# Score bursts of two head pairs, an earlier Exp table load, one maximum per head and another list order in a two-layer encoder kernel

## Chip, cores and metric

The kernel runs on one core of a Trainium2 chip. The metric is the device time of one execution in microseconds (us); lower is better.

## What is computed

Two layers, each a mixer and a channel part, on x of 256 tokens by 1024 features, in float32. The mixer has 16 heads of width 64 in three kinds: four neighbourhood heads ("a", with a relative position bias), six dilated window heads ("d") and six heads ("c") that share two key and value heads.

```python
def mixer_sublayer(x, n1, w_in_l, qg, kg, rpb_l, og, w_out_l, tables):
    h = rms_norm(x, n1)
    proj = h @ w_in_l                         # 1024 x 2560
    qa, ka, va, qd, kd, vd, qc, kc, vc = jnp.split(proj, cuts, axis=-1)
    # q and k: rms_norm per head, rotary positions for d and c
    out_a = neighbourhood_attention(...)
    out_d = dilated_window_attention(...)
    out_c = gqa_block_attention(...)
    mix = concatenate([rms_norm(out_a), rms_norm(out_d), rms_norm(out_c)])
    return x + mix @ w_out_l                  # 1024 x 1024

def channel_sublayer(x, n2, w_gu, cw, cb, w_dn):
    h = rms_norm(x, n2)
    g, u = jnp.split(h @ w_gu, 2, axis=-1)    # 1024 x 5632
    g = depthwise_conv_centred(g, cw, cb)     # width 3 along the tokens
    return x + (jax.nn.gelu(g) * u) @ w_dn    # 2816 x 1024

for l in range(2):
    x = mixer_sublayer(...)
    x = channel_sublayer(...)
```

## The kernel before

Tokens lie on the 128 partitions in two tiles (t = 0, 1); their transposes, features on partitions, are what TensorE multiplies. Every float32 product is three matmuls (`mm3`): each operand is split into a high and a low part, and high·high, high·low and low·high are added up in PSUM. So each weight that arrives (`wp_raw`) is cast to its high part by ScalarE (`wp_hi`) and subtracted to its low part by VectorE (`wp_lo`) before TensorE can use it. Weights come in units of up to 2048 columns; four raw buffers and two pairs of parts exist. The first unit u0 of layer 0 comes in four slices w0 to w3 of 128 features each, the second in two halves u1a and u1b of 256 features (together the eight k-steps of the first group of projections), u2 and u3 whole. x comes in five pieces: x(k, n) is the feature blocks k to k+n-1 for all tokens, and x(0,1) and x(1,1) go by ScalarE's queue. Everything else goes by SyncE's (SP's) queue, in the order in which SP issues it.

Stages of a layer: transposes of x into `act_hT` (scaled by the norm's gain, split by ScalarE and VectorE, the form with two operands on VectorE being the low part), the projections in groups (dq, dk, ... into the four PSUM tiles `psa_a`), sums of squares per head (`act_s2k` from `psa_a`, `small_ss`), rotary positions, then the heads. A head's steps are: scores into one PSUM tile "w" of 256 keys for both token tiles (the pool `psw` has four such tiles), a maximum (VectorE), Exp with a row sum (ScalarE), the transposes of p back through `psw`, a split into `act_ch` and `act_cl`, and the weigh step against `const_v`. Scores of two heads are computed in one burst, one head on the lower 64 rows of the array and one on the upper (`scores`, with `nc.together()`: nothing may come between). Projections of later groups are woven in as filler. Then come the three group norms (`act_sqm` is transposed for their sums), the output matrix with `act_mixT_hi` and `act_mixT_lo`, and the addition to `const_x`. The channel part walks through eleven steps of gate (G), up (U) and down; four PSUM tiles `dacc[t][h]` gather the down products for token tile t and column half h, and the last addition writes x out. At the start TensorE multiplies some constants (`const_warm`) while it waits.

No instruction is issued where it is written. `Plan.add` records each operation, and `Plan.order` then sets the order of the whole program by list scheduling: it follows estimated durations (`cost`), estimated DMA times and buffer handovers, and always takes the operation that can start earliest, with ties by rank. The rank is the recorded position, plus shifts of whole sections (`later`), plus an entry of the table `PLACES` for single operations. The first thirteen DMAs, those of the list `START`, have fixed landing times in the table `LANDS`, which are taken by their recorded position:

```python
o.rank = i + self.shift + PLACES.get(i, 0)
...
if i < self.first_loads:
    end = LANDS[sum(p.method == "dma_start" for p in ops[:i])]
```

`not_before(engine)` records that an operation must stand behind the last one recorded so far on that engine. Since all are issued in one helper, every line of the trace is L470; tiles tell the operations apart.

Of the kernel before, what the change touches and what calls it, by code (L numbers as in the profile page):

```python
# [224 lines left out]
def handover(a, b):  # L225
# [1 line left out]


PLACES = {
# [5 lines left out]
}  # L235


class Plan:
    def __init__(self, tc):
        self.tc, self.ops, self.shift, self.burst, self.bursts, self.behind = tc, [], 0, None, {}, None  # L240
# [28 lines left out]
    def add(self, engine, method, args, kw):  # L269
# [49 lines left out]
    def order(self):  # L319
# [79 lines left out]
        while len(done) < len(ops):  # L399
            best = None  # L400
            for e, r in ready.items():
                for i in r:
                    o = ops[i]
                    if e in opened:
                        if o.burst != opened[e]:
                            continue
                        at = at_of(o)
                    elif o.burst is not None:
                        at = at_of_burst(o.burst) if i == self.bursts[o.burst][0] else None
                    else:  # L410
# [25 lines left out]
            if o.method == "dma_start":  # L436

                ring = e if i < self.first_loads else "SP"
                end = max(at + 1360, wires.get(ring, 0.0))
                shared = 0.0  # L440
                if i < self.first_loads:
                    shared = o.size if ring == "ACT" else min(o.size, 120 * max(0.0, wires.get("ACT", 0.0) - end))
                if e == "POOL":
                    end += 1000
                wires[ring] = end + shared / 120 + (o.size - shared) / (280 if i < self.first_loads else 335)
                end = wires[ring] + 1200
                if i < self.first_loads:
                    end = LANDS[sum(p.method == "dma_start" for p in ops[:i])]
            for t in o.tiles:
# [23 lines left out]
def cost(engine, method, args, kw, ins):  # L473

    out = args[0]
    if method == "dma_start":
        w = out if isinstance(out, View) else args[1]
        small = min(out.shape[-1], args[1].shape[-1]) < 128
        spread = isinstance(args[1], bass.AP) and args[1].ap[0][0] == 0
        size = 4 * math.prod(w.shape) * (2 if small else 2 if spread else 1)  # L480
# [34 lines left out]
def encoder_kernel(  # L515
# [72 lines left out]

    minus_half = const.tile([P, 32], F32, tag="mh", name="minus_half")
    nc.gpsimd.memset(minus_half, -0.5)  # L590


    vown, vkv = (
# [281 lines left out]
    for l in range(DEPTH):  # L875
# [181 lines left out]
        class Head:  # L1057
# [4 lines left out]
            def softens(self, sps):  # L1062
# [142 lines left out]
        def na_bias(h):  # L1205

            flat = nabs[l].rearrange("p r c -> p (r c)")
            return [flat[:, (h * RPB_ROWS + 3 - 2 * t) * GRID_W :][:, :S] for t in range(NT)]

        def scores(i):  # L1210

            two = heads[i : i + 2]
            sps = [psw.tile([P, NT, S], F32, tag="w", name=f"s_{z.name}") for z in two]
            g = two[0].group
            with nc.together():
                for t in range(NT):
                    for x, y in ((0, 0), (0, 1), (1, 0)):
                        for z, sp, rows_ in zip(two, sps, (LOW, HIGH)):
                            nc.tensor.matmul(
                                sp[:, t], turned[g + "q"][x][rows_, z.h // 2, t * P : (t + 1) * P],  # L1220
                                turned[g + "k"][y][rows_, z.kv if g == "c" else z.h // 2],
                                start=(x, y) == (0, 0), stop=(x, y) == (1, 0),
                            )
            for z, sp in zip(two, sps):
                z.softens([sp[:, t] for t in range(NT)])

        heads = []
        for h in range(H_DIL):
# [144 lines left out]
        def gate(s):  # L1373
# [28 lines left out]
        def down(steps):  # L1402
            ws = [unit() for _ in steps]
            for h in range(2):
                hs = slice(h * 512, (h + 1) * 512)
                for t in range(NT):
                    c = slice(t * P, (t + 1) * P)
                    for s, (wh, wl) in zip(steps, ws):
                        ch, cl = ready[s]
                        for j in range(2):  # L1410
                            mm3(
                                dacc[t][h], ch[:, j, c], cl[:, j, c], wh[:, j, hs], wl[:, j, hs],
                                s == 0 and j == 0, s == STEPS - 1 and j == 1,
                            )

        last = []
        NA_STEPS = {2: na_load, 3: na_repeat, 4: na_diagonals}
# [19 lines left out]
        for h in range(2):  # L1437
            for t in range(NT):
                hs = slice(h * 512, (h + 1) * 512)
                nc.vector.scalar_tensor_tensor(  # L1440
                    xs[:, t, hs], dacc[t][h], r2[:, t : t + 1], xs[:, t, hs], ALU.mult, ALU.add
                )
                if l == DEPTH - 1:
                    nc.sync.dma_start(ov[:, t, hs], xs[:, t, hs])
    nc.emit()


# [67 lines left out]
```

## Time and profile before

| | before |
|---|---|
| median of 3 runs | 614.73 us (614.57 to 614.73) |
| profiled execution | 614.38 us, span 612.6 us |
| granted TensorE clock, mean | 1.00 |
| layer 0: start, mixer, channel | 0 to 13.9, to 122.3, to 309.7 us |
| layer 1: mixer, channel, tail | to 423.2, to 608.6, to 612.6 us |
| TensorE (PE) busy | 604.5 us |
| VectorE (DVE), ScalarE (ACT) busy | 485.4, 428.5 us |
| GpSimd (POOL) busy | 84.3 us |

The profile is one execution; its span is the time from the first to the last recorded instruction. A row of a timeline gives the start, the duration, the engine, the operation with its output and inputs, shapes, and in brackets the idle time before it with what ended it. A row that stands for several instructions has their count at its end (x8) and the time from the first's start to the last's end. A row of windows gives the window, its length, the busy time of PE, PEld (weight load), DVE, ACT and POOL with counts, the granted clock, the share of DMA time and GB/s. Groups have count, busy us, mean ns and idle us. "SPq" is SyncE's issue of a DMA.

### The profile page before, as it was taken

To read this page: it belongs to the slowest core of one execution; us is meant where nothing else is said; L and a number is where in the kernel's file an instruction comes from. 1 tells how busy PE (TensorE), PEld (TensorE's weight loads), DVE (VectorE), ACT (ScalarE), POOL (GpSimd) and SP (SyncE) were. 2 spreads that over 40 slices of the span, in tenths; PEclk is the share of its full clock that TensorE was granted. 3 is DMA by queue.
4 is the path that set the end of the run, shared out by engine and by line. 5 is a ranking of instruction groups with operands and counts; after the bars stand their busy time and mean duration, and the time that the engine had idled before them with its cause. 6 is when DMAs were issued, how large, how long until landed. Compare 5 with 4: busy or idle time off the path is not lost.

```text
span 612.6 us, 9883 instructions
## 1 busy us (share of the span) xinstructions
PE 604.5 (99%) x3484; PEld 525.2 (86%) x3484; DVE 485.4 (79%) x1000; ACT 428.5 (70%) x1064; POOL 84.3 (14%) x136
## 2 busy tenths in 40 slices
PE   8999999999999999999999999998999999999997
PEld 6998888888888888888899989887888888888885
DVE  4899989797788988887777788767877777777774
ACT  6789999696565766675588889857755656566661
POOL 2732130202400000000032214231000000000000
PEclk9999999999999999999999999999999999999999
DMA  8893403557589799987555626654665555556501
GB/s 272 294 294 141 139 25 105 184 159 242 166 225 326 247 360 326 349 293 251 155 155 182 215 70 240 206 178 129 202 217 179 175 197 201 167 185 205 189 18 68
DMA packets 85073, 121.44 MB, mean 198 GB/s; under 512 B 9864, under 2 KB 69608, under 8 KB 85024
## 3 DMA queue, kind: packets, MB, share of 16 engines
q1 hardware_dynamic: 82752, 112.17, 56.6%
q0 software_dynamic: 1728, 8.39, 4.0%
q8 instruction: 27, 0.44, 0.3%
q10 hardware_dynamic: 544, 0.26, 0.2%
q14 instruction: 22, 0.18, 0.1%
HBM read 110.93 MB, written 9.88 MB: 197 GB/s over the span
## 4 chain that ended last, share of the span: by engine, by line
PE 92%; DVE 2%; ACT 2%; POOL 1%; DMA 1%; issue 1%; SPq 0%; DVEq 0%; POOLq 0%
PE psw_w L470 51%; PE psa_a L470 41%; DMA const_x<-in_x_dram 1%; ACT act_s2k L470 1%; POOL small_rstd L470 1%; DVE const_x L470 1%; DVE wp_lo L470 1%; SPq L470 0%; DVE act_sw L470 0%; DVE act_z L470 0%; ACT wp_hi L470 0%; POOL small_ms L470 0%; ACT L470 0%; ACT act_z L470 0%; ACT act_hT L470 0%
## 5 line engine op out<-in xcount | busy, mean ns | idle before, releaser
L470 DVE TENSOR_TENSOR wp_lo<-wp_raw,wp_hi 128x512 fp32r<-128x512 f32 (+2 forms) x332 | 232.1, 735 | 53.9 <-ACT wp_hi L470 36.8
L470 ACT CAST wp_hi<-wp_raw 128x512 fp32r<-128x512 f32 (+2 forms) x332 | 202.5, 663 | 21.7 <-PE psa_a L470 9.1
L470 PE MATMUL psw_w<-act_hT,wp_hi 128*128 128x512 f32 x704 | 181.4, 393 | 0.0
L470 PEld LDWEIGHTS psw_w<-act_hT,wp_hi 128*128 128x128 f32 x704 | 128.1, 189 | 24.7
L470 PE MATMUL psa_a<-wp_hi,act_hT 128*128 128x384 f32 (+2 forms) x448 | 113.3, 332 | 0.5 <-ACT wp_hi L470 0.5
L470 PEld LDWEIGHTS psw_w<-act_hT,wp_lo 128*128 128x128 f32 x704 | 97.9, 190 | 6.9
L470 PE MATMUL psw_w<-act_hT,wp_lo 128*128 128x256 f32 x704 | 102.8, 282 | 0.0
L470 PEld LDWEIGHTS psa_a<-wp_hi,act_hT 128*128 128x128 f32 x448 | 78.1, 189 | 4.0 <-ACT wp_hi L470 0.8
L470 PE MATMUL psa_a<-wp_lo,act_hT 128*128 128x384 f32 (+2 forms) x224 | 74.2, 333 | 0.3 <-DVE wp_lo L470 0.2
L470 ACT COPY act_s2k<-psw_w 128x256 f32<-128x256 f32 x88 | 32.2, 371 | 58.7 <-PE psw_w L470 58.5
L470 PE MATMUL psa_a<-wp_lo,act_ch 128*128 128x512 f32 x176 | 69.4, 394 | 0.0
L470 PE MATMUL psa_a<-wp_hi,act_cl 128*128 128x512 f32 x176 | 69.4, 395 | 0.0
L470 PE MATMUL psa_a<-wp_hi,act_ch 128*128 128x512 f32 x176 | 68.9, 394 | 0.0
L470 DVE TENSOR_TENSOR act_s2k<-psw_w,act_s2k 128x256 f32<-128x256 f32 x88 | 36.7, 422 | 15.2 <-ACT act_s2k L470 14.9
L470 PEld LDWEIGHTS psa_a<-wp_lo,act_hT 128*128 128x128 f32 x224 | 42.2, 188 | 3.0 <-DVE wp_lo L470 1.7
L470 PEld LDWEIGHTS psa_a<-wp_hi,act_cl 128*128 128x128 f32 x176 | 33.2, 188 | 7.9 <-DVE act_cl L470 0.3
L470 PEld LDWEIGHTS psa_a<-wp_hi,act_ch 128*128 128x128 f32 x176 | 33.2, 189 | 6.7
L470 PEld LDWEIGHTS psa_a<-wp_lo,act_ch 128*128 128x128 f32 x176 | 33.1, 188 | 6.8
L470 DVE SCALAR_TENSOR_TENSOR act_s2k<-act_s2k,act_cw,act_s2k 128x255 f32<-128x255 f32 x88 | 36.8, 482 | 1.4 <-ACT act_s2k L470 1.3
L470 ACT ACTIVATE act_s2k<-act_s2k,act_cw 128x256 f32<-128x256 f32 x44 | 24.1, 595 | 18.0 <-DVE act_s2k L470 18.0
L470 ACT ACTIVATE act_s2k<-act_s2k 128x512 f32<-128x512 f32 x22 | 13.9, 631 | 30.0 <-DVE act_s2k L470 30.0
L470 POOL TENSOR_TENSOR small_rstd<-small_ms,const_mh 128x6 f32<-128x6 f32 (+2 forms) x26 | 31.7, 1218 | 2.2
(112 smaller groups left out, 794.7 us busy)
## 6 DMA issues: line engine op xcount, KB each, us to landing
wp_raw<-in_w_gate_up_dram SPq DMA_DIRECT2D x44, 1024.0 KB, 5.2
wp_raw<-in_w_down_dram SPq DMA_DIRECT2D x22, 1024.0 KB, 5.0
wp_raw<-in_w_in_dram SPq DMA_DIRECT2D x14, 768.0 KB, 6.3
wp_raw<-in_w_in_dram SPq DMA_DIRECT2D x8, 1024.0 KB, 8.8
wp_raw<-in_w_out_dram SPq DMA_DIRECT2D x8, 768.0 KB, 9.5
dram_khi<-act_mixT_hi SPq DMA_DIRECT2D x4, 768.0 KB, 9.5
dram_klo<-act_mixT_lo SPq DMA_DIRECT2D x4, 768.0 KB, 9.8
wp_lo<-dram_klo POOLq DMA_DIRECT2D x4, 768.0 KB, 5.4
```

The costliest lines, as they stand in the source:

```text
L470: getattr(o.engine.real, o.method)(*map(real, o.args), **{k: real(v) for k, v in o.kw.items()})
```

## The change

1. The list order: `LANDS` has other numbers, `PLACES` other entries (those of before all go; the new ones begin with the constants and first loads, positions 39 to 171), `cost` and the DMA estimates are changed, a table of loaded activation functions is followed, and equal ranks go by position.
2. `BURSTS`: heads 0 to 3, 6 to 9 and 12 to 15 are scored four to a burst (24 half-row matmuls, all four `psw` tiles), the pairs 4 and 10 alone as before. So a layer has five bursts in place of eight.
3. `softens`: one maximum over both token tiles (128x512) in place of one for each (128x256), which serves both.
4. Behind the last Gelu of layer 0 ScalarE runs Exp on one column of a constant (`few_out`), so that the Exp table is loaded there.
5. In layer 1 the last down group (h, t) = (1, 1) is split into columns 512 to 767 and 768 to 1023, the second in a tile "end" of `psw`, each with an addition and an output DMA of its own.

```diff
-LANDS = (4074, 3054, 5167, 3987, 5363, 6065, 7002, 7704, 8406, 9342, 10278, 10308, 10337)
+LANDS = (4100, 3300, 5300, 3450, 5800, 6450, 7250, 8200, 8900, 9800, 10700, 10750, 10800)
...
 PLACES = {
-    715: 185, 722: 185, 772: -261, 980: -22, 982: -95, 983: -95, 1039: -192, 1146: -2, 1150: -159, 1350: 23,
...
+    39: 195, 40: 195, 42: 239, 43: -54, 44: 239, 45: -61, 46: -256, 69: -132, 107: -53, 108: -53, 109: -53,
+    119: -79, 120: -79, 121: -79, 124: 41, 168: -360, 169: -191, 170: -210, 171: -193, 252: 101, 255: 101, 267: 8,
...
+        func = args[2] if method == "activation" else None
+        if func in (AF.Exp, AF.Gelu) and func != self.table:
+            self.table, o.ns, o.lat = func, o.ns + 1290, o.lat + 1290
...
-                    if at is not None and (best is None or (at, o.rank) < best[:2]):
+                    if at is not None and (best is None or (at, o.rank, i) < best):
...
-                if e == "POOL":
-                    end += 1000
-                wires[ring] = end + shared / 120 + (o.size - shared) / (280 if i < self.first_loads else 335)
-                end = wires[ring] + 1200
+                wires[ring] = end + shared / 120 + (o.size - shared) / (280 if i < self.first_loads else 360)
+                end = wires[ring] + 1000
...
-                    for t in range(NT):
-                        nc.vector.reduce_max(nm[:, t : t + 1], sps[t], axis=AX.X, negate=True)
+                nc.vector.reduce_max(nm, whole, axis=AX.X, negate=True)
...
+        BURSTS = {0: 2, 4: 1, 6: 2, 10: 1, 12: 2}
+        scored = {}
...
-            two = heads[i : i + 2]
-            sps = [psw.tile([P, NT, S], F32, tag="w", name=f"s_{z.name}") for z in two]
-            g = two[0].group
-            with nc.together():
-                for t in range(NT):
...
+            if i in BURSTS:
+                with nc.together():
+                    for n in range(i, i + 2 * BURSTS[i], 2):
+                        two = heads[n : n + 2]
+                        sps = [psw.tile([P, NT, S], F32, tag="w", name=f"s_{z.name}") for z in two]
+                        scored[n] = sps
...
+            for z, sp in zip(heads[i : i + 2], scored[i]):
+                z.softens([sp[:, t] for t in range(NT)], sp)
...
             nc.scalar.activation(B, A, AF.Gelu)
             made[s] = B
+            if s == STEPS - 1 and l + 1 < DEPTH:
+                with nc.not_before("ACT"):
+                    nc.scalar.activation(few_out, minus_half[:, :1], AF.Exp)
...
+                    halved = l == DEPTH - 1 and steps[-1] == STEPS - 1 and (h, t) == (1, 1)
+                    if halved:
+                        end = psw.tile([P, S], F32, tag="w", name="end")
+                    for a, b in ((512, 768), (768, 1024)) if halved else ((hs.start, hs.stop),):
...
+        if l == DEPTH - 1:
+            hs = slice(768, 1024)
+            nc.vector.scalar_tensor_tensor(xs[:, 1, hs], hold["end"], r2[:, 1:2], xs[:, 1, hs], ALU.mult, ALU.add)
+            nc.sync.dma_start(ov[:, 1, hs], xs[:, 1, hs])
```

What stands in a row, at the places where the order moves most. First the first DMAs on SP's queue. `const_x` are pieces of x, `wp_raw` of shape 128x384 a slice w0 to w3, 128x2x384 the halves u1a and u1b, 128x4x384 the units u2 and u3; before:

```order
L470 DMA const_ident_89<-in_c_ident_dram 128x128
L470 DMA wp_raw_95<-in_w_in_dram 128x384 x2
L470 DMA const_x_79<-in_x_dram 128x2x256
L470 DMA wp_raw_95<-in_w_in_dram 128x384 x2
L470 DMA const_x_79<-in_x_dram 128x2x256 x2
L470 DMA act_s2k_131<-in_out_norm_g_dram 16x128
L470 DMA act_s2k_131<-in_norm_g_dram 16x128
L470 DMA wp_raw_141<-in_w_in_dram 128x2x384 x2
L470 DMA wp_raw_155<-in_w_in_dram 128x4x384
L470 DMA wp_raw_164<-in_w_in_dram 128x4x384
L470 DMA const_rot_174<-in_c_rot_dram 128x2x208
```

After, eight DMAs stand ahead of these rows: the rotary table (208 KB), the key and query gains (192 KB each), `act_few` (3.4 KB), the x piece x(4,2) (256 KB) and three norm gains (8 KB each). Then:

```order
L472 DMA const_ident_125<-in_c_ident_dram 128x128
L472 DMA wp_raw_134<-in_w_in_dram 128x384 x2
L472 DMA wp_raw_148<-in_w_in_dram 128x2x384 x2
L472 DMA wp_raw_164<-in_w_in_dram 128x4x384
L472 DMA wp_raw_173<-in_w_in_dram 128x4x384
L472 DMA wp_raw_134<-in_w_in_dram 128x384
L472 DMA const_x_81<-in_x_dram 128x2x256
L472 DMA wp_raw_134<-in_w_in_dram 128x384
L472 DMA const_x_81<-in_x_dram 128x2x256
L472 DMA const_dil_211<-in_c_dil_dram 128x2x256
```

The slice w1, the piece x(2,2), w3 and x(6,2) have moved behind u1a, u1b, u2 and u3 (384, 384, 768 and 768 KB).

The same place on ScalarE (casts of weight slices, `act_hT` for the transposes of x, squares of x with `const_x` as input), before:

```order
L470 CAST wp_hi_136<-wp_raw_95 128x384
L470 ACTIVATE act_hT_143<-psw_w_122,const_gains_127 128x256
L470 CAST wp_hi_136<-wp_raw_95 128x384
L470 ACTIVATE act_hT_143<-psw_w_122,const_gains_127 128x256
L470 ACTIVATE act_s2k_168,small_ssx_167<-const_x_79 128x512
L470 CAST wp_hi_136<-wp_raw_95 128x384
L470 ACTIVATE act_hT_143<-psw_w_162,const_gains_127 128x256
L470 CAST wp_hi_136<-wp_raw_95 128x384
L470 ACTIVATE act_s2k_193,small_ssx_167<-const_x_79 128x512
L470 ACTIVATE act_hT_143<-psw_w_162,const_gains_127 128x256
L470 ACTIVATE act_hT_143<-psw_w_120,const_gains_127 128x256 x2
```

After:

```order
L472 CAST wp_hi_150<-wp_raw_134 128x384
L472 ACTIVATE act_hT_157<-psw_w_131,const_gains_137 128x256 x2
L472 CAST wp_hi_150<-wp_raw_134 128x384
L472 ACTIVATE act_s2k_190,small_ssx_189<-const_x_81 128x512
L472 ACTIVATE act_s2k_192,small_ssx_189<-const_x_81 128x512
L472 CAST wp_hi_150<-wp_raw_134 128x384
L472 ACTIVATE act_hT_157<-psw_w_194,const_gains_137 128x256
L472 CAST wp_hi_150<-wp_raw_134 128x384
L472 CAST wp_hi_216<-wp_raw_148 128x384
L472 ACTIVATE act_hT_157<-psw_w_194,const_gains_137 128x256
L472 CAST wp_hi_216<-wp_raw_148 128x384 x3
L472 ACTIVATE act_hT_157<-psw_w_127,const_gains_137 128x256 x2
```

The squares of two x pieces, which need x(2,2), stand right behind the cast of w1 and ahead of the casts of w2, w3 and u1, the last pieces of hT behind the casts of u1.

The end of layer 1's mixer on PE, between the last weigh step (`act_ch`, `const_v`) and the transposes of the new x (`const_ident`, `const_x`). Before, from the norm's transposes on (eight 512-column matmuls stand between the weigh step and this):

```order
L470 MATMUL psw_w_162<-const_ident_89,act_sqm_1010 128x128 x2
L470 MATMUL psw_w_122<-const_ident_89,act_s2k_221 128x88
L470 MATMUL psa_a_153<-wp_hi_136,act_mixT_lo_886 128x512
L470 MATMUL psa_a_159<-wp_hi_136,act_mixT_hi_870 128x512
L470 MATMUL psa_a_159<-wp_lo_248,act_mixT_hi_870 128x512
L470 MATMUL psa_a_159<-wp_hi_136,act_mixT_lo_886 128x512
L470 MATMUL psw_w_120<-const_ident_89,const_x_79 128x128
L470 MATMUL psw_w_83<-const_ident_89,const_x_79 128x128
L470 MATMUL psw_w_120<-const_ident_89,const_x_79 128x128 x3
```

After (sixteen 512-column matmuls stand between the weigh step and this):

```order
L472 MATMUL psw_w_194<-const_ident_125,act_sqm_968 128x128 x2
L472 MATMUL psw_w_83<-const_ident_125,act_s2k_115 128x88
L472 MATMUL psa_a_176<-wp_hi_216,act_mixT_hi_866 128x512
L472 MATMUL psa_a_169<-wp_hi_216,act_mixT_hi_866 128x512
L472 MATMUL psa_a_176<-wp_hi_216,act_mixT_hi_866 128x512
L472 MATMUL psa_a_176<-wp_lo_228,act_mixT_hi_866 128x512
L472 MATMUL psa_a_176<-wp_hi_216,act_mixT_lo_920 128x512
L472 MATMUL psw_w_127<-const_ident_125,const_x_81 128x128 x4
```

Between the fourth and the fifth of these rows stand seven more matmuls of 512 columns with `act_mixT`: twelve in all between the norm's transposes and those of x, where before there are four.

The last additions on DVE in layer 1, one for each down group, before:

```order
L470 TENSOR_TENSOR act_cl_829<-act_s2k_131,act_ch_811 128x512
L470 SCALAR_TENSOR_TENSOR const_x_79<-psa_a_153,small_rx_1588,const_x_79 128x512
L470 SCALAR_TENSOR_TENSOR const_x_79<-psa_a_159,small_rx_1588,const_x_79 128x512
L470 SCALAR_TENSOR_TENSOR const_x_79<-psa_a_327,small_rx_1588,const_x_79 128x512
L470 SCALAR_TENSOR_TENSOR const_x_79<-psa_a_299,small_rx_1588,const_x_79 128x512
```

After:

```order
L472 TENSOR_TENSOR act_cl_829<-act_s2k_111,act_ch_822 128x512
L472 SCALAR_TENSOR_TENSOR const_x_81<-psa_a_176,small_rx_1580,const_x_81 128x512
L472 SCALAR_TENSOR_TENSOR const_x_81<-psa_a_326,small_rx_1580,const_x_81 128x512
L472 SCALAR_TENSOR_TENSOR const_x_81<-psa_a_359,small_rx_1580,const_x_81 128x512
L472 SCALAR_TENSOR_TENSOR const_x_81<-psw_w_127,small_rx_1580,const_x_81 128x256
L472 SCALAR_TENSOR_TENSOR const_x_81<-psa_a_169,small_rx_1580,const_x_81 128x512
```

The group of `psa_a_359` and `psw_w_127` is the halved one, and the whole group `psa_a_169` stands behind it; PE computes them in the same order.

More of the change, by code (lines that the diff above doesn't have):

```diff
@@ L239, in __init__ @@
     def __init__(self, tc):
-        self.tc, self.ops, self.shift, self.burst, self.bursts, self.behind = tc, [], 0, None, {}, None
+        self.tc, self.ops, self.shift, self.burst, self.bursts, self.behind, self.table = tc, [], 0, None, {}, None, AF.Exp
         for name, short in (("tensor", "PE"), ("scalar", "ACT"), ("vector", "DVE"), ("gpsimd", "POOL"), ("sync", "SP")):
@@ L479, in cost @@
         spread = isinstance(args[1], bass.AP) and args[1].ap[0][0] == 0
-        size = 4 * math.prod(w.shape) * (2 if small else 2 if spread else 1)
+        stored = isinstance(out, View) and out.tile.pool.dram
+        size = 4 * math.prod(w.shape) * (2 if small or spread else 1.5 if stored else 1)
         return 620 if engine == "POOL" else 480, 0, size, None
@@ L590, in encoder_kernel @@
     nc.gpsimd.memset(minus_half, -0.5)
+    few_out = const.tile([P, 1], F32, tag="fo", name="few_out")
     vown, vkv = (
@@ L1208, in na_bias @@
             return [flat[:, (h * RPB_ROWS + 3 - 2 * t) * GRID_W :][:, :S] for t in range(NT)]
+        BURSTS = {0: 2, 4: 1, 6: 2, 10: 1, 12: 2}
+        scored = {}
         def scores(i):
[L1212 to L1225 removed]
+            if i in BURSTS:
[4 more added lines that the diff above has]
+                        scored[n] = sps
+                        g = two[0].group
+                        for t in range(NT):
+                            for x, y in ((0, 0), (0, 1), (1, 0)):
+                                for z, sp, rows_ in zip(two, sps, (LOW, HIGH)):
+                                    nc.tensor.matmul(
+                                        sp[:, t], turned[g + "q"][x][rows_, z.h // 2, t * P : (t + 1) * P],
+                                        turned[g + "k"][y][rows_, z.kv if g == "c" else z.h // 2],
+                                        start=(x, y) == (0, 0), stop=(x, y) == (1, 0),
+                                    )
+            for z, sp in zip(heads[i : i + 2], scored[i]):
+                z.softens([sp[:, t] for t in range(NT)], sp)
         heads = []
@@ L1407, in down @@
                     c = slice(t * P, (t + 1) * P)
[L1408 to L1414, printed above, removed]
+                    halved = l == DEPTH - 1 and steps[-1] == STEPS - 1 and (h, t) == (1, 1)
+                    if halved:
+                        end = psw.tile([P, S], F32, tag="w", name="end")
+                    for a, b in ((512, 768), (768, 1024)) if halved else ((hs.start, hs.stop),):
+                        for s, (wh, wl) in zip(steps, ws):
+                            ch, cl = ready[s]
+                            for j in range(2):
+                                apart = a == 768
+                                mm3(
+                                    end if apart else dacc[t][h][:, : b - a],
+                                    ch[:, j, c], cl[:, j, c], wh[:, j, a:b], wl[:, j, a:b],
+                                    (s == 0 or apart and s == steps[0]) and j == 0, s == STEPS - 1 and j == 1,
+                                )
+                    if halved:
+                        hold["end"] = end
         last = []
```

9 lines of the change are left out of this document (6 added, 3 removed), and 8 rows, old and new, of the table PLACES.

## The prediction

> **What bounds the kernel now.** I read the page's busy times, then the waits of TensorE (PE), the chain that ended last, and timelines where PE waits.
>
> ```profile
> PE 604.5 (99%) x3484; PEld 525.2 (86%) x3484; DVE 485.4 (79%) x1000; ACT 428.5 (70%) x1064; POOL 84.3 (14%) x136
> ...
> PE psw_w L470 <- DVE const_x L470: 1.6, 2, 1.3
> ...
> PE psw_w L470 <- ACT act_s2k L470: 0.5, 1, 0.5
> ...
> 597.45 11.17 PE psa_a L470 x48
> ```
>
> PE is busy 99%: every microsecond must come out of PE's own work or out of its waits (total us, count, longest us). The largest wait between the first matmul and the tail is 1.3 us. So a change can win little, and anything that starves PE costs in full. A 512-column matmul runs at 11.17/48 = 0.233 us.
>
> **The start.** The diff moves the first loads. All of them lie on one queue, in order.
>
> ```profile
> wp_raw<-in_w_in_dram SPq DMA_DIRECT2D x5, 768.0 KB, 9.2
> wp_raw<-in_w_in_dram SPq DMA_DIRECT2D x4, 192.0 KB, 4.1
> const_x<-in_x_dram SPq DMA_DIRECT2D x3, 256.0 KB, 4.1
> ...
> 0.00:8.00 8.00, 7.00 (x39) 5.17 (x40) 1.96 (x5) 3.45 (x6) 2.73 (x10) 1.00 0.72 211
> 8.00:12.00 4.00, 3.95 (x26) 3.41 (x25) 2.54 (x7) 3.76 (x12) 0.00 (x0) 1.00 0.94 305
> 12.00:15.30 3.30, 2.81 (x15) 1.93 (x15) 2.80 (x8) 3.30 (x11) 1.49 (x4) 1.00 1.07 382
> 15.30:16.00 0.70, 0.70 (x6) 0.70 (x5) 0.70 (x3) 0.70 (x3) 0.20 (x1) 1.00 1.08 368
> ...
> 4.04 5.93 DMA const_x<-in_x_dram
> ```
>
> The last column of the windows is GB/s: 1.69 MB are moved by 8.0 us, 2.91 by 12.0, 4.17 by 15.3 and 4.43 by 16.0. The times to landing (4.1 us for 192 KB, 9.2 us for 768 KB) are times in a queue, so a load lands when the bytes ahead of it have moved. The new order puts the second weight slice w1 and the x piece x(2,2) behind u1 to u3, 2304 KB, and behind the rotary table and the two key and query gains. From the sizes, 4075 KB (4.17 MB) end with w1 and 4331 KB (4.43 MB) with x(2,2). On the record of before they have moved at 15.3 and 16.0 us.
>
> ```profile
> 5.24 0.51 ACT L470 CAST wp_hi<-wp_raw 128x384 fp32r<-128x384 f32 x1 [2.23 <-DMA wp_raw<-in_w_in_dram]
> 10.01 0.42 PEld L470 LDWEIGHTS psw_w<-const_ident,const_x 128*128 128x128 f32 x4 [0.37 <-DMA const_x<-in_x_dram]
> 12.05 0.83 ACT L470 ACTIVATE act_hT<-psw_w,const_gains 128x256 fp32r<-128x256 f32 x2
> 12.76 0.64 ACT L470 ACTIVATE act_s2k<-const_x 128x512 f32<-128x512 f32 x1
> 12.92 0.88 DVE L470 SCALAR_TENSOR_TENSOR act_hT<-psw_w,const_gains,act_hT 128x256 fp32r<-128x256 f32 x2 [0.46 <-ACT act_hT L470]
> 13.38 3.49 ACT L470 CAST wp_hi<-wp_raw 128x384 fp32r<-128x384 f32 x8
> 13.92 3.84 DVE L470 TENSOR_TENSOR wp_lo<-wp_raw,wp_hi 128x384 fp32r<-128x384 f32 x8
> 18.66 0.23 ACT L470 ACTIVATE act_s2k<-psa_a 128x64 f32<-128x64 f32 x1
> ```
>
> Use follows the move: w0 (0.53 MB, 2.5 us at 211 GB/s, some 4.2 with the idle head) is cast at 5.24, lag 1.0 us; x(4,2) (1.65 MB, 7.9 us) is used at 10.01, lag 2.1. With 1.5, w1 is there at 16.8 and x(2,2) at 17.5.
>
> PE's order needs w1's casts for the second k-step, and ACT's order puts behind that cast two Squares that read x(2,2), and behind those every later cast. So at 17.5 ACT still has two Squares (0.64 each), six casts (3.49/8 = 0.44 each) and six hT (0.83/2 = 0.42 each): 1.28 + 2.62 + 2.49 = 6.4, that is 23.9. DVE's lo half of the last hT follows 0.8 us later, 24.7 (its own 0.48 and 0.44 per piece keep pace). Then ten 384-column matmuls (0.175 each, from the timeline below) stand before the sums of the second token tile: 26.5, where before has them at 18.66. **The start costs +7.8 us.** Bounds: 2.74 MB after the first 1.69 at 382 GB/s with lag 1.0 give +6.5; if the first 8 us too moved 305 GB/s, 0.75 MB more, +4.5. Lag 2.1 gives +8.4, a slow PE on top +10. The two x pieces, the table and the gains that go ahead move work of GpSimd (14% busy) forward, which PE never waits for: 0. What PE idles in the rest of layer 0's attention can be caught up, since loads and other engines are then ahead of it: 103.34 − 102.91 in the window below, −0.4 (0 to −0.4).
>
> ```profile
> 18.29 0.51 PE L470 MATMUL psa_a<-wp_hi,act_hT 128*128 128x384 f32 x2
> 18.64 0.33 PE L470 MATMUL psa_a<-wp_lo,act_hT 128*128 128x384 f32 x1
> ...
> 18.66:122.00 103.34, 102.91 (x685) 91.16 (x684) 92.16 (x238) 88.06 (x286) 34.09 (x51) 1.00 0.53 163
> ```
>
> **Bursts.** Sixteen score bursts become ten.
>
> ```profile
> 73.00 0.28 PE L470 MATMUL psw_w<-act_ch,const_v 128*128 128x256 f32 x1
> 73.20 0.98 PE L470 MATMUL psw_w<-act_kc,act_qc 64*128 64x256 f32 x12
> 74.11 0.38 PE L470 MATMUL psa_a<-wp_hi,act_hT 128*128 128x256 f32 x1
> 74.33 0.28 PE L470 MATMUL psa_a<-wp_lo,act_hT 128*128 128x256 f32 x1
> 74.45 0.60 PE L470 MATMUL psw_w<-const_ident,act_s2k 128*128 128x128 f32 x4
> ```
>
> A 256-column matmul takes 0.12 (74.33 to 74.45). From 73.00 to 74.33 are 1.33 us; less two of these and less six pairs on the two halves of the rows (0.71), 0.38 is what going to half rows and back costs. Six fewer: −2.3; I take **−1.9**, since a burst beside a transpose saves less (down to −1.5). New is that one burst takes all four "w" PSUM tiles, so that transposes and weigh steps behind it wait until DVE and ACT have read scores: **+0.5** (0 to +3, four heads' Exp at 0.64 us each beside the 2.9 us of other matmuls that PE's order puts behind a burst).
>
> **Exp table.** Before, it is loaded at the first Exp of layer 1.
>
> ```profile
> 345.90 0.65 ACT L470 CAST wp_hi<-wp_raw 128x512 fp32r<-128x512 f32 x1
> 346.57 1.28 ACT L470 ACT_TABLE_LOAD   x1
> 350.45 0.33 PE L470 MATMUL psw_w<-const_ident,act_s2k 128*128 128x128 f32 x1 [0.50 <-ACT act_s2k L470]
> ...
> 296.38 0.39 PE L470 MATMUL psa_a<-wp_hi,act_ch 128*128 128x512 f32 x1
> ...
> 297.83 0.62 ACT L470 COPY act_s2k<-psw_w 128x256 f32<-128x256 f32 x2
> ...
> 300.50 0.62 ACT L470 CAST act_ch<-act_s2k 128x512 fp32r<-128x512 f32 x1 [2.06 <-DVE act_s2k L470]
> ```
>
> The load takes 1.28 us and PE's wait of 0.50 goes: **−0.5** (0 to −1.28). In its new place ACT runs it between the two COPYs at 297.83, behind which DVE's two additions and the cast at 300.50 wait. Delayed by 1.5 it ends at 302.6 at the latest; PE needs it after 24 matmuls from 296.38, 24 × 0.233 = 301.98: cover all but gone, 0 to +0.6, taken 0. The load at 346.57 follows a cast that ended at 346.55 (345.90 + 0.65): no drain is to be seen.
> The Trainium skill, ScalarE: Activation LUTs, section "What ACT_TABLE_LOAD costs", says that every switch costs a drain of about 1380 ns besides the 1283 ns of the load; by it this place would cost some 1.4 us more. The trace agrees with the load's length and not with a drain ahead of it.
>
> **End of layer 1's attention.**
>
> ```profile
> 414.11 0.28 PE L470 MATMUL psw_w<-act_ch,const_v 128*128 128x256 f32 x1
> ...
> 418.85 0.44 PE L470 MATMUL psw_w<-const_ident,const_x 128*128 128x128 f32 x2 [1.33 <-DVE const_x L470]
> ```
>
> Between the last weigh step (414.11) and the transposes of x stand 12 matmuls (2.8 us), while the chain over sums, norm and residual takes 4.6. The new order has 28 there (6.5 us), 16 of them ahead of the norm's transposes: the wait goes, **−1.3** (0 to −1.6, both waits of the first list).
>
> **One maximum.** 24 reductions of 256 columns become 12 of 512 columns:
>
> ```profile
> L470 DVE TENSOR_REDUCE small_nm<-psw_w 128x1 f32<-128x256 f32 x24 | 8.8, 419 | 0.3
> ...
> 608.64 0.75 DVE L470 SCALAR_TENSOR_TENSOR const_x<-psa_a,small_rx,const_x 128x512 f32<-128x512 f32 x1 [1.11 <-PE psa_a L470]
> ```
>
> The twelve take at most what the 24 took, 8.8 us, on an engine that is 79% busy and hidden by PE: 0, though the first Exp of a head can start up to 0.42 later, which is in the cost of the bursts' waits.
>
> **The tail.** The halved group is placed ahead of another group that is still whole, so the last addition is again 512 columns (0.75 us at 608.64) with one output DMA behind: 0, and +0.05 for 12 matmuls of 512 columns that become 24 of 256.
>
> **Sum.** +7.8 − 0.4 − 1.9 + 0.5 − 0.5 − 1.3 + 0 + 0.05 = +4.25. The profiled execution took 614.38, 0.35 below the median of the runs, 614.73; on the median that is **619.0 us**.
>
> **Rivals.**
> *Order of the queue doesn't decide (faster).* If a load's time hangs on its own issue and not on the bytes ahead, w1 and x(2,2) are there when PE comes to them. It decides from the point where both land about when they do before: the start costs 0, nothing is caught up, and −1.9 + 0.5 − 0.5 − 1.3 + 0.05 gives 611.6. For it: loads of 192 and of 256 KB show the same 4.1 us. Against: 9.2 us for 768 KB. 7%.
> *PE comes back slow.* After the long wait the ten matmuls go at the pace of the first warming ones:
>
> ```profile
> 0.98 3.60 PE L470 MATMUL psw_w<-const_warm 128*128 128x256 bf16 x16 [0.98 <-POOL const_warm L470]
> ...
> 5.99 0.71 PE L470 MATMUL psw_w<-const_warm 128*128 128x256 bf16 x5
> ```
>
> 0.225 us each against 0.142: ten lose 1.0 us and the catch-up of 0.4 is lost: 620.4. The granted clock (1.00 in all windows above) shows no fall, but no wait of that length either. 18%. The Trainium skill, TensorE: Matmul & The Clock Gate, section "What's actually happening", has PE at half rate after an idle window of some 3.4 us; by it the ten would lose 1.75.
> *Four tiles at once.* The waits behind double bursts come to +3 in place of +0.5: 621.5. For it: all "w" tiles are taken; against: PE's order has 2.9 us of other work behind each. 13%.
> *The loads are quicker*, +4.5 in place of +7.8: 615.7. For it: the early windows are slow because little is queued. 12%.
> That the change doesn't do what it says holds for the last group in halves, and is in the sum.
>
> **Numbers.** Forecast 50%. A difference below 0.2% (1.2 us) can't be told from none. Faster 0.07 (the first rival), same 0.07 and slower 0.05 out of the quick loads, the rest slower: 0.86. The range reaches from the quick loads to the four tiles with the upper start, 615.2 to 622.5.
>
> **What would show it.** Right: PE idle for 5 us or more between 8 and 18 us, ended by ACT's cast of w1; the first sums of the second token tile near 26; no table load ahead of layer 1's first Exp; no wait for x at the end of layer 1's attention; a last addition of 0.75 us. Wrong: w1 cast before 12 us, or a wait of over 1 us at PE behind double bursts in both layers.

## The result: 622.19 us, 1.2% slower

The changed kernel takes 622.19 us (median of 4 runs, 621.32 to 623.16) against 614.67 for before (median of 4 runs); the ratio is 1.0124, 95% interval [1.0108, 1.0140]. That is +7.5 us where +4.3 was forecast, inside the range. The profiled execution took 622.40 us. From its page, and the answer on PE's waits (total us, count, longest):

```profile
span 620.6 us, 9909 instructions
PE 605.5 (98%) x3496; PEld 529.4 (85%) x3496; DVE 482.7 (78%) x989; ACT 427.8 (69%) x1065; POOL 80.9 (13%) x136
...
PE psa_a L472 <- ACT wp_hi L472: 5.9, 1, 5.9
PE psw_w L472 <- DMA const_ident<-in_c_ident_dram: 3.3, 1, 3.3
PE psw_w L472 <- POOL const_warm L472: 1.0, 1, 1.0
PE psw_w L472 <- DVE const_x L472: 0.8, 1, 0.8
```

Two waits stand at the head that before did not have: 3.3 us for the identity and 5.9 us for the cast of w1. PE's timeline and ScalarE's show both, and windows (length, then busy us of PE, PEld, DVE, ACT and POOL, granted clock, DMA share, GB/s) show what followed:

```profile
0.98 4.02 PE L472 MATMUL psw_w<-const_warm 128*128 128x256 bf16 x18 [0.98 <-POOL const_warm L472]
8.30 0.28 PE L472 MATMUL psw_w<-const_ident,act_s2k 16*128 16x16 f32 x1 [3.29 <-DMA const_ident<-in_c_ident_dram]
...
12.63 0.52 PE L472 MATMUL psa_a<-wp_hi,act_hT 128*128 128x384 f32 x1
19.03 1.01 PE L472 MATMUL psa_a<-wp_hi,act_hT 128*128 128x384 f32 x2 [5.88 <-ACT wp_hi L472]
...
18.46 0.51 ACT L472 CAST wp_hi<-wp_raw 128x384 fp32r<-128x384 f32 x1 [7.32 <-DMA wp_raw<-in_w_in_dram]
...
0.00:8.00 8.00, 4.02 (x18) 2.55 (x18) 0.00 (x0) 1.28 (x1) 4.50 (x17) 1.00 0.69 168
...
17.00:20.40 3.40, 1.37 (x5) 1.28 (x6) 0.56 (x1) 1.75 (x5) 0.00 (x0) 0.50 0.92 326
20.40:23.80 3.40, 3.40 (x14) 3.09 (x13) 2.87 (x7) 3.38 (x10) 0.00 (x0) 0.53 0.15 27
23.80:28.00 4.20, 4.20 (x29) 4.17 (x28) 2.61 (x7) 3.33 (x11) 0.36 (x2) 1.00 0.96 286
```

PE stands still from 13.2 to 19.0 us, and then has half its clock until 23.6 us: 14 matmuls in 3.4 us, where the next 4.2 us hold 29. The table follows the loss through the program by the start of the same matmul in each trace (us; differences from before):

| start of | before | changed | loads_as_before | best |
|---|---|---|---|---|
| 48th projection matmul, layer 0 | 18.29 | +11.66 | −0.30 | +0.21 |
| 100th | 27.40 | +12.32 | +1.99 | +1.75 |
| last output matmul, layer 0 | 121.91 | +9.92 | +0.52 | +0.29 |
| first projection matmul, layer 1 | 309.47 | +9.82 | +0.45 | +0.20 |
| last output matmul, layer 1 | 422.77 | +7.71 | −1.72 | −1.89 |
| last matmul | 608.20 | +8.12 | −1.34 | −1.36 |

Nearly all of the loss is there by the 48th projection matmul, which stands at 18.29 us in before and at 29.96 us in the change. Each layer's mixer behind it is about 2 us faster than before.

### The profile page after: what moved, and what is told of

Its sections match the earlier page's. It is cut to its first block, busy times and chain, and to the rows that moved or that the text cites. A ratio compares the mean times of both kernels' runs of the same rounds, so it can differ in the third digit from the quotient of the medians.

```text
span 620.6 us, 9909 instructions
## 1 busy us (share of the span) xinstructions
PE 605.5 (98%) x3496; PEld 529.4 (85%) x3496; DVE 482.7 (78%) x989; ACT 427.8 (69%) x1065; POOL 80.9 (13%) x136
## 4 chain that ended last, share of the span: by engine, by line
PE 95%; DMA 3%; SPq 0%; DVE 0%; issue 0%; POOL 0%; ACT 0%; POOLq 0%
PE psw_w L472 50%; PE psa_a L472 45%; DMA wp_raw<-in_w_in_dram 1%; DMA wp_hi<-dram_khi 1%; DMA const_gq<-in_q_norm_g_dram 1%; SPq L472 0%; DVE const_x L472 0%; POOL act_sqm L472 0%; ACT wp_hi L472 0%; POOL wp_lo L472 0%; POOLq L472 0%
## 5 line engine op out<-in xcount | busy, mean ns | idle before, releaser
L472 PE MATMUL psa_a<-wp_hi,act_hT 128*128 128x384 f32 (+2 forms) x448 | 116.4, 338 | 5.9 <-ACT wp_hi L472 5.9
L472 PEld LDWEIGHTS psa_a<-wp_hi,act_hT 128*128 128x128 f32 x448 | 80.0, 192 | 9.1 <-ACT wp_hi L472 6.4
L472 PE MATMUL psa_a<-wp_lo,act_hT 128*128 128x384 f32 (+2 forms) x224 | 75.8, 339 | 0.0
L472 PE MATMUL psa_a<-wp_lo,act_ch 128*128 128x512 f32 (+1 forms) x176 | 69.0, 392 | 0.0
L472 PE MATMUL psa_a<-wp_hi,act_cl 128*128 128x512 f32 (+1 forms) x176 | 68.4, 392 | 0.0
L472 ACT ACTIVATE act_s2k<-act_s2k,act_cw 128x256 f32<-128x256 f32 x44 | 24.1, 595 | 15.3 <-DVE act_s2k L472 15.3
```

What stands on the lines that cost most here:

```text
L472: getattr(o.engine.real, o.method)(*map(real, o.args), **{k: real(v) for k, v in o.kw.items()})
```

## Experiments

**The order of the first loads.** Three kernels take shifts out of the table; none of the three moves PE beyond its first 250 matmuls.

```diff
# loads_as_before: without
-    39: 195, 40: 195, 42: 239, 43: -54, 44: 239, 45: -61, 46: -256, 69: -132, 107: -53, 108: -53, 109: -53,
-    119: -79, 120: -79, 121: -79, 124: 41, 168: -360, 169: -191, 170: -210, 171: -193,
# w1_early: without 39, 40, 42, 44 alone
# ident_early: without 43, 45, 46, 168, 169, 170, 171 alone
```

> The change with its shifts of recorded positions 39 to 171 taken out, so that the first loads come in the order of before; behind PE's first 219 matmuls nothing moves. Theory (the order of the loads costs the time): PE's hundredth projection matmul, 12.3 us late in the trace of the changed kernel, is on time, and the run takes 622.2 - 12 = 610 us, or up to 612 where the 2 us that layer 0 made up were a catch-up. Rival (the loads hide, the loss lies in the later order): 618 us or more.

Measured 613.53 us (ratio to before 0.9987 [0.9978, 0.9996]), 8.7 us less than the change: the loads cost it, and the rest of the change is a small gain. The 48th matmul is on time. But by the hundredth 2.0 us are lost again, and only part comes back: the forecast of 610 to 612 was too low by 1.5 us.

> Only w1, x(2,2), w3 and x(6,2) go back ahead of u1 to u3; the rotary table, the gains and x(4,2) still go ahead of the identity. Theory (two waits, 4.5 us at the start for the identity and w0, the rest for w1): the first remains, 610.2 + 4.5 = 614.7 us. Rival (w1 alone costs it all, the first wait is made up): 610 to 611 us.

Measured 616.74 us (1.0039 [1.0024, 1.0054]), 3.2 us above loads_as_before. PE still waits 3.6 us for the identity, and its 48th matmul is 4.4 us late: the first theory, of two waits with 4.5 us for the first, holds for the start. Against loads_as_before it is 4.7 us late at the 48th and 3.4 us late at the hundredth, so 1.3 us is made up in between (here `act_few` still comes early; what that is worth follows below).

> Only the identity, w0 and the small loads keep their old place; w1 and x(2,2) stay behind u1 to u3 and behind the table and gains, so the bytes ahead of them are the same. Theory (a load lands when the bytes ahead have moved, the first wait hides in the second): w1 still comes at about 18 us, and the run takes 621 to 622 us. Rival (the two waits add): 622.2 - 4.5 = 617.7 us.

Measured 623.05 us (1.0144 [1.0129, 1.0160]): no gain at all, though the identity's wait is gone. All of it went into the other wait, and a new one of 1.2 us came:

```profile
PE psa_a L472 <- ACT wp_hi L472: 10.2, 1, 10.2
PE psa_a L472 <- DVE wp_lo L472: 1.2, 1, 1.2
```

w1 is cast at 17.67 us (18.46 in the change): it comes when the bytes ahead of it have moved, whatever else is early. The rival, that the waits add, falls.

**The clock.** Constant matmuls are issued again ahead of the first one that needs w1 (recorded position 104).

```diff
+                for o in [self.ops[i]] if i != 104 else [self.ops[1]] * 28 + [self.ops[i]]:
```

> The changed kernel with 28 more constant matmuls on PE in the long wait for w1 (3 us at full pace, 6 us at half), all else in its place. Theory (PE comes back at half clock and that costs time): the granted clock stays near 1 from 17 to 28 us, the matmuls behind the wait are 0.175 us apart and not 0.32, and the run takes 620.2 us. Rival (the casts of ScalarE and VectorE set the pace there): 622.2 us.

Measured 621.28 us (1.0110 [1.0093, 1.0126]), 0.9 us less than the change, but the two intervals overlap. The 28 matmuls ended at 15.3 us and a wait of 2.8 us was left; PE's waits and the windows show it:

```profile
PE psa_a L472 <- ACT wp_hi L472: 2.8, 1, 2.8
...
17.00:20.00 3.00, 1.92 (x9) 1.88 (x10) 0.56 (x1) 2.05 (x6) 0.00 (x0) 0.81 0.82 284
20.00:28.00 8.00, 8.00 (x45) 7.66 (x45) 6.84 (x15) 7.76 (x28) 1.68 (x4) 0.86 0.65 195
```

The 48th matmul came 1.5 us earlier, but 0.9 of that is w1, which in this trace is cast at 17.52 us with the loads in the same order. Three traces together say more. From the end of the wait for w1 to the 48th projection matmul PE runs the same matmuls without a wait in the change (10.93 us), in kept_warm (10.41) and in ident_early (10.75), and has half its clock for 4.54, 3.41 and 4.10 us of that. Less half of these times, 8.7 us are left in each. So the half clock cost PE 2.3 us in the change, and the casts did not set the pace. At full clock they might; a full cover was not run.

**What loads_as_before still loses.** Its landing-time table was put back first.

```diff
# loads_lands_before: loads_as_before, and
-LANDS = (4100, 3300, 5300, 3450, 5800, 6450, 7250, 8200, 8900, 9800, 10700, 10750, 10800)
+LANDS = (4074, 3054, 5167, 3987, 5363, 6065, 7002, 7704, 8406, 9342, 10278, 10308, 10337)
```

> The first loads as in before and also the old landing times in the table, so that PE's first 127 instructions are those of before; the rest of the change stays (layer 0's mixer is ordered anew, layer 1 is as in the change). Theory: with the first loads alone as in before, PE lost 2.0 us by its hundredth projection matmul (a wait of 1.2 us for a low weight part at 24 us); that goes, and the run takes 613.5 - 2 = 611.5 us. Rival (layer 0 makes those 2 us up by its end anyway): 613.5 us.

Measured 615.97 us (1.0033 [1.0024, 1.0042]): worse, and the theory falls. The wait for the low weight part grew to 1.5 us. That is not all of the 2.4 us: another 1.0 us is lost at the start of layer 0's channel part, where PE now waits 0.7 us for `act_hT`. PE's waits, and VectorE's and GpSimd's timelines, of loads_as_before give another cause:

```profile
PE psa_a L472 <- DVE wp_lo L472: 1.2, 1, 1.2
...
21.55 0.55 DVE L472 TENSOR_TENSOR wp_lo<-wp_raw,wp_hi 128x384 fp32r<-128x384 f32 x1
...
23.65 2.19 DVE L472 TENSOR_TENSOR wp_lo<-wp_raw,wp_hi 128x384 fp32r<-128x384 f32 x1
...
23.55 1.87 POOL L472 COPY act_nab<-act_few 28x1984 f32<-28x1984 f32 x1
```

The same subtraction takes 0.55 us alone and 2.19 us while GpSimd copies `act_few` into `act_nab`; it ends 0.4 us behind the COPY. In before the COPY runs from 24.52 us and meets a rotary step that PE does not wait for. In loads_lands_before, too, the COPY (from 24.63 us) meets such a step, of 1.95 us, and the subtraction that PE waits for stands right behind it. In the change `act_few` came early and the COPY, from 7.79 us, was over by then: the new load order had a gain of its own. The Trainium skill, SBUF — State Buffer, section "SBUF: two separate sides", says why: VectorE, with two SBUF inputs, and GpSimd, when it reads SBUF, hold a shared port in turn for a whole instruction. The trace agrees: those 0.4 us behind the COPY are about what the subtraction takes alone.

```diff
# few_early: loads_as_before, with one shift left in
+    171: -193,
```

> The kernel loads_as_before, but the 3.4 KB of the position bias (act_few) go first on SP's queue, so that GpSimd's COPY of it into act_nab (1.87 us, at 23.55 in the trace of loads_as_before) runs in the first microseconds. Theory (VectorE's subtraction for a low weight part, which took 2.19 us beside that COPY where others take 0.55, is held up by it, and PE waits 1.2 us for it): PE's hundredth projection matmul comes 1.2 to 1.9 us earlier than in loads_as_before and the run takes 613.5 - 1.5 = 612 us. Rival (the subtraction is slow for another reason, such as its weights arriving): no change, 613.5 us.

Measured 616.37 us (1.0034 [1.0022, 1.0047]): slower, against both. The mechanism was there: PE's wait for the subtraction fell from 1.16 to 0.32 us, and from the 48th to the 100th matmul it took 10.70 us in place of 11.38. But at 41 us a new wait of 1.0 us for a low weight part takes that gain back, and two costs came with it. SP issues the load first, and the identity waits:

```profile
0.72 0.84 SPq L472 DMA_DIRECT2D act_few<-in_rpb_dram  x1
1.62 0.39 SPq L472 DMA_DIRECT2D act_s2k<-in_norm_g_dram  x1
2.05 0.42 SPq L472 DMA_DIRECT2D const_ident<-in_c_ident_dram  x1
```

And all matmuls that read `act_hT` became slower. Groups by form of few_early, then of loads_as_before (count | busy us, mean ns | idle):

```profile
L472 PE MATMUL psw_w<-act_hT,wp_hi 128*128 128x512 f32 x704 | 182.2, 396 | 0.0
...
L472 PE MATMUL psa_a<-wp_lo,act_ch 128*128 128x512 f32 x172 | 67.8, 394 | 0.0
```

```profile
L472 PE MATMUL psw_w<-act_hT,wp_hi 128*128 128x512 f32 x704 | 180.4, 393 | 0.0
...
L472 PE MATMUL psa_a<-wp_lo,act_ch 128*128 128x512 f32 x172 | 67.8, 394 | 0.0
```

Start to start, the 512-column ones from `act_hT` are 0.232 us apart in place of 0.230, those from `act_ch` are unchanged. Both kernels run the same matmuls, and behind PE's first 220 in the same order; what differs is the order in which tiles first appear, and by that their places in SBUF.

```diff
# best: few_early without 5569: 82, with 171: -130 in place of -193, and
+            for name in "<tiles of act and const in the order of loads_as_before>".split():
+                tiles[name].pool.place(tiles[name])
...
-        nc.sync.dma_start(
+        (nc.scalar if l == 0 else nc.sync).dma_start(      # act_few, third on ScalarE's queue
```

> The kernel few_early_half_last, but the position bias goes as the third load of ScalarE's queue (so that it no longer takes 0.84 us of SP's issue ahead of the identity), and the tiles get their places in SBUF in the order of loads_as_before, not in that of few_early. Theory (few_early lost 0.8 us to the later identity and x, and some 2.3 us since its matmuls that read act_hT were 1% slower with other places of the tiles): both go, and with the COPY of GpSimd out of the way (0.7 us from the 48th to the 100th projection matmul) and the halved group last (0.4 us or nothing) the run takes 613.5 - 0.7 to 613.5 - 1.1 = 612.4 to 612.8 us; the 512-column matmuls from act_hT come 0.230 us apart as in loads_as_before, not 0.232. Rival (the slower matmuls have another cause, such as the chip): 615 us or more.

Measured 611.98 us (610.85 to 612.46), ratio to before 0.9952 [0.9935, 0.9970]: faster than both kernels, and below the expected 612.4 to 612.8. The matmuls from `act_hT` are 0.230 us apart again. Of the edits only the places of the tiles reach them: without the entry 5569 alone (few_early_half_last, below) they keep 0.232, and the chip is no rival, since before took 614.45 us beside few_early and 614.35 beside loads_as_before. So the places were the cause; what about the places, was not tried. The rest of the theory did not hold. The early position bias won nothing in the end: the wait for the subtraction is 0.3 us, but the next one, for `act_z`, grows from 0.2 to 1.3 us, and the last matmul stands at 606.84 us where loads_as_before has it at 606.86. The two traces differ by 0.5 us, at the end of the program; the other 1.0 us between the two medians, which were taken at separate times, is not explained.

**Bursts.** In loads_lands_before's own order, the second pair of each double burst is issued eight PE instructions later.

```diff
+                second = burst[12:]
+                ...                      # eight PE instructions later in the list
```

> The kernel loads_lands_before in its own order, but in each double burst the 12 matmuls of the second pair stand some PE instructions later, so that 10 bursts become 16. Theory (a burst costs 0.3 to 0.38 us of going to half rows and back): 6 x 0.3 to 6 x 0.38 = 1.8 to 2.3 us slower than loads_lands_before. Rival (what the bursts save is lost again to waits for four PSUM tiles): no difference.

Measured 618.85 us against 615.97: 2.9 us slower. In the traces 0.5 us of it lies ahead of the hundredth projection matmul, where both issue the same; from there to the last matmul it is 2.3 us, the upper end of the theory. The prediction's measure of a burst (from the start of the matmul ahead of it to the start of the second one behind it, less the usual pace of what runs in between) gives 4.0 us for ten bursts and 6.4 for sixteen, without the wait of 0.5 us in one: 0.39 us for each of the six. New waits for maxima (`small_nm`, 2 waits, 0.9 us) come on top, since the second pair's scores come later, and other waits shrink. The saving is real, and PE's waits have none for a PSUM tile behind a burst.

**Exp table.** Same order, the Exp on the constant left out.

```diff
+                if o.method == "activation" and o.args[0].shape[1] == 1 and o.args[0].tile.pool.tag == "fo":
+                    continue
```

> The kernel loads_lands_before in its own order, without the Exp on the constant, so that the Exp table is loaded at layer 1's first Exp as before. Theory: PE's wait of 0.5 us there comes back, 0.5 us slower than loads_lands_before. Rival (the early load delays the last down products of layer 0 by as much, or nobody waits for either): no difference. By the Trainium skill, ScalarE: Activation LUTs, section 'What ACT_TABLE_LOAD costs', each switch costs a drain besides the load; it would then be 1.4 us more wherever it stands in PE's way.

Measured 617.98 us against 615.97, but its runs lie from 616.04 to 618.30 and by the hundredth matmul, up to which both issue the same, the two traces differ by 0.9 us (last section). Four of its five runs have a granted clock of 0.997 or less, but only four of the eleven of loads_lands_before; the median of such runs is 618.1 against 617.3, and the one other run of late_table has 616.04 against 615.9. The traces tell more: PE's wait for the first Exp is back with 0.3 us, and layer 1's mixer, from its first projection matmul to its last output matmul, takes 111.9 us in place of 111.5 (111.6 in half_last, which issues the same there). So 0.2 to 0.4 us for the early load. Layer 0's channel part takes the same in both. There is no drain beside the load in the changed kernel either; the instructions ahead of it and behind it follow without a pause:

```profile
307.73 0.35 ACT L472 COPY act_s2k<-psw_w 128x256 f32<-128x256 f32 x1
308.10 1.28 ACT L472 ACT_TABLE_LOAD   x1
309.39 0.20 ACT L472 ACTIVATE const_fo<-const_mh 128x1 f32<-128x1 f32 x1
309.50 0.35 ACT L472 COPY act_s2k<-psw_w 128x256 f32<-128x256 f32 x1
```

**The last group, and the maxima.**

```diff
# half_last, few_early_half_last: without
-    5569: 82,
# two_maxima: few_early, and for each maximum in its place
+                if o.method == "reduce_max" and len(o.args[1].shape) == 3:
+                    for t in range(NT):
+                        o.engine.real.reduce_max(real(o.args[0][:, t : t + 1]), real(o.args[1][:, t]), **o.kw)
+                    continue
```

> The kernel loads_lands_before without the entry 5569 of the table of shifts, so that the halved group is PE's last and no whole group stands behind it. Theory: the last addition has 256 columns (0.42 us in place of 0.75) and the last output DMA half the bytes: 0.4 to 0.6 us faster than loads_lands_before. Rival (the end is set by the output DMA's fixed time): 0.3 us or less.

> The kernel few_early without the entry 5569 of the table of shifts, so that the halved group of the last layer is PE's last. From the trace of half_last, whose stretch from the last up matmul to the end was 0.4 us shorter than that of loads_lands_before: 0.4 us faster than few_early. Rival (a difference between two single traces that is noise): none.

Measured 615.92 against 615.97, and 616.18 against 616.37 us. The runs do not separate them. In the traces the stretch from the start of the last up matmul to the end is 15.0 us in both (and in best), and 15.4 in every trace with the whole group last. So about 0.4 us, read from traces alone.

> The kernel few_early in its own order, but each maximum over both token tiles is taken as two, one for each tile, in the same place. Theory (VectorE is hidden by PE): within 0.3 us of few_early. Rival (VectorE's 2 us count where heads wait for their Exp): 0.5 to 1 us slower.

Measured 617.16 against 616.37 us, with overlapping runs, and 0.9 us of the difference arises between the 48th and the 100th matmul, ahead of any maximum. Behind that, the two mixers together are 0.5 us longer. The one maximum is worth half a microsecond at most.

## Why the prediction came out as it did

The sum was 3.3 us short of the measured +7.5, and the step that was mis-sized is the start.

- **The start, +7.8: right in kind, too small.** Queue order decided, as loads_as_before and ident_early show. By the 48th matmul it cost 11.7, and the first sums of the second token tile stand at 30.33 us and not near 26. Two things were mis-sized. The first is w1, cast at 18.46 and not at 16.8, 1.7 us later: I took the bytes of before's record, but with the new order only 168 GB/s moved in the first 8 us (before 211). Two causes are at hand, and no run separates them. From 4 to 6 us the DMA engines were busy throughout (share 1.10 and 1.00), yet moved only 200 GB/s, where before moved 298. And SP spends 0.35 to 0.83 us on issuing each load, and the identity is the ninth:

```profile
0.73 0.43 SPq L472 DMA_DIRECT2D const_rot<-in_c_rot_dram  x1
...
5.52 0.35 SPq L472 DMA_DIRECT2D const_ident<-in_c_ident_dram  x1
```

The second is the clock. The rival of a slow PE, which I set apart with 18%, came on top of the forecast, with another price: it had 1.0 us for ten matmuls at 0.225, but PE, busy without a pause behind the wait, had half its clock for 4.5 us and lost 2.3 us.
- **The identity** was no term of its own. It cost 3.3 us of waiting, hidden by the wait for w1: in ident_early that wait takes it over.
- **GpSimd's work moved forward, 0: wrong.** From the 48th projection matmul to PE's 221st matmul of any kind the change takes 21.9 us and loads_as_before 24.2. Some 1.2 of these 2.3 us are the COPY of `act_nab`, which in the change no longer met a subtraction that PE waits for: ident_early, with the loads as late as in the change but `act_few` where before has it, has the subtraction of 2.19 us beside the COPY again (35.59 and 35.48 us), waits 1.2 us for it and takes 23.1 us. The rest is not explained. This is why taking the loads back gained 8.7 and not 11.7.
- **Catch-up, −0.4: about right.** Behind its 221st matmul PE runs the same order in both, and by the end of layer 0's mixer the change makes up 0.3 us on loads_as_before.
- **Bursts, −1.9: right.** By the measure above the sixteen bursts of before cost 6.1 us and the ten of the change 4.0: −2.1 in all. The four taken tiles cost nothing (+0.5 forecast).
- **Exp table, −0.5: right in kind** (0.2 to 0.4), and free in its new place.
- **End of layer 1's mixer, −1.3: mis-sized.** A wait stayed:

```profile
419.02 0.29 PE L472 MATMUL psw_w<-act_ch,const_v 128*128 128x256 f32 x1
422.87 0.38 PE L472 MATMUL psw_w<-const_ident,act_sqm 128*128 128x128 f32 x2
...
427.00 0.77 PE L472 MATMUL psw_w<-const_ident,const_x 128*128 128x128 f32 x5 [0.84 <-DVE const_x L472]
```

I set 28 matmuls (6.5 us) against a chain of 4.6 from the last weigh step. But the chain runs through the norm's transposes on PE, and these now stand behind 16 matmuls, 3.85 us behind the weigh step and not 1.98. From there it takes 4.1 us, with 2.8 us of matmuls to cover it. The gain is 1.55 − 0.84 = 0.7.
- **Maximum and tail, 0 and +0.05: right, as far as the runs tell** (the maximum to half a microsecond). The last addition is whole and takes 0.75 us:

```profile
616.75 0.75 DVE L472 SCALAR_TENSOR_TENSOR const_x<-psa_a,small_rx,const_x 128x512 f32<-128x512 f32 x1 [1.35 <-PE psa_a L472]
```

- **Not explained:** layer 1's channel part, where the change loses another 0.4 us.
- **Luck.** Behind the 48th projection matmul the traces give −3.7 us, and the terms for this part add up to −3.55. The sum is closer than its terms: the gain at the end of the mixer was half of the forecast and layer 1's channel part lost 0.4, while the +0.5 for the tiles did not come and the COPY gave 1.2.

## What to carry to other kernels

A load's time is its place in the queue, by the bytes ahead of it: a scheduler with fixed landing times for its first loads is free to move them, and will, at no cost that it can see. Where one engine is 99% busy, look first at what starves it, and add to each wait what the engine loses when it comes back. When a chain passes through the busy engine itself, count the cover from each of its steps there, not from its head.

## What the runs showed of the hardware

**A wait of 1.5 us can halve the clock, in some runs.** late_table and loads_lands_before issue the same instructions here, and PE waits 1.48 us for the same subtraction in both. Windows of late_table, then of loads_lands_before:

```profile
27.00:28.00 1.00, 0.93 (x5) 0.93 (x6) 1.00 (x3) 0.00 (x0) 1.00 (x3) 0.88 0.39 140
28.00:31.00 3.00, 3.00 (x12) 2.88 (x11) 1.85 (x5) 0.88 (x2) 1.97 (x6) 0.50 0.23 45
```

```profile
28.00:31.00 3.00, 3.00 (x19) 2.71 (x19) 2.68 (x7) 1.07 (x3) 2.45 (x7) 1.00 0.09 23
```

12 matmuls against 19: from the 48th to the 100th projection matmul late_table takes 14.0 us and loads_lands_before 12.3, so the slow stretch cost 1.7 us, half of its length. half_last, with the same instructions there, has it too. The runs of loads_lands_before fall into two groups, near 615.9 us with a granted clock of 0.999 or 1.000 and near 617.3 us with 0.997. The Trainium skill, TensorE: Matmul & The Clock Gate, section "What's actually happening", has the clock fall after an idle window of about 3.4 us that runs freely; the length of the slow stretch agrees (some 3.4 us), the idle time that was enough is shorter here (1.48 us).

**Places of tiles in SBUF** changed the pace of the matmuls that read one of them by 1% (0.232 against 0.230 us), some 2 us of the kernel, with the same instructions.
